# State space steps over pairs of groups, later row stores and earlier B and C loads in a hybrid decoder layer

## Chip, cores and metric

One core of a Trainium2 chip. The metric is the device time of one execution in microseconds (us). It was 2678.44 us before the change, the median of 3 runs (2677.90 to 2678.88).

## What is computed

One decoder layer on 2048 tokens of width 1024, in fp32. The input is normalised and projected by one matrix; the columns go to three mixers (sliding-window attention, a state space model, sparse attention). Their outputs are normalised, projected and added; a feed-forward block follows. The change touches the projection and the state space model alone:

```python
h = rms_norm(x, norm1_g[l]); proj = jnp.einsum('bld,de->ble', h, w_in[l])
# s5_mixer: 32 groups of 16 channels, 64 complex states per group
A_bar = jnp.exp(A * dt); B_bar = ((A_bar - 1.0) / A)[..., None] * Bm
Bu = jnp.einsum('blgp,gnp->blgn', uf, B_bar)
_, states = lax.associative_scan(_scan_combine, (a_seq, Bu), axis=1)
y = jnp.einsum('blgn,gpn->blgp', states, Cm).real + d_skip * uf
z = jax.nn.gelu(y)          # then a gated linear unit
```

## The kernel before

`phase_front` (L82) projects and runs the state space model; it ends at about 489 us, and attention and the rest follow. Sixteen blocks of 128 tokens are taken in two halves of eight. `load_h` loads and splits a block and starts a chain of 128x1 operations on POOL (L45 to L50), which gives the row scale r. `load_w` loads a chunk of weight columns in four pieces (wr, L130) and splits them on ACT (wh, L136) and DVE (wl, L137). `product` (L146) multiplies one block by one chunk: 24 matmuls into pm, three for each of 8 slices (`mm3`, L77 to L79). A product of a u chunk is scaled by r into u_st (L156). One of an a or c chunk goes to po (L160), with sums of squares beside it, and from there to memory at once (pa L166, pc L169); po has two buffers. pm has two buffers too, so PE opens a third product only when ACT has emptied the first.

In half 0 `ssm_tables` (L256) runs beside the products. It loads B (t_B, L371 to L374) and, two parts later, C (craw, L394 and L395, sixteen loads into four buffers), which PE transposes (L396). In half 1 the u products come first. Then `merge` (L65) interleaves 68 steps of the other chunks, most of them half a product of 12 matmuls, evenly with the 65 steps of `ssm_steps`. That order is written out: engines run their instructions in it, each waiting in its own queue.

`ssm_steps` (L414) works for each of the 32 groups g. On POOL `kernel_of` makes CA (L444 to L446, 128x272), an outer product of powers and C, for group g+2. PE then makes the local kernel pk (L448), which ACT and DVE copy to kst, and SP stores it (dkp, L453). `turned` loads CS (CA with its halves exchanged, L465, L466) and Wc (a shifted reading of dkp), and transposes B and u (pbt L481, pu L487). `scanned` multiplies into pv (L498); then DVE rotates (m, L501, L502) and scans (Q, L504), and POOL rotates back (St, L506). `answer` sums into py, two matmuls from Wc and two from St (L512 to L515), and gelu writes u_st (L516). For each g the order is turned(g+1), scanned(g), answer(g-1).

Of the kernel before, what the change touches and what calls it, by code (L numbers as in the profile page):

```python
# [16 lines left out]
P = 128  # L17
D = 1024
# [63 lines left out]
def phase_front(tc, C, x, norm1_g, w_in, u_st, pa, pc, rh_a, prm, dkp, extra):  # L82

    nc = tc.nc
    with ExitStack() as ctx:
# [15 lines left out]
        def load_h(s):  # L101
# [41 lines left out]
        def product(s, hs, w, kind, c0, n, part=None):  # L143
# [13 lines left out]
            else:  # L157
                f, nh = HEADS[c0]
                o = sp.tile([P, n + nh], F32, tag="po", name=f"po{s}_{c0}")
# [13 lines left out]
        for half in range(2):  # L173
# [14 lines left out]
            with tc.tile_pool(name=f"a_x{half}", bufs=2, reuse_waits="tile") as xp:  # L188
                box_x[:] = [xp]
                run(lists[0] + (lists[1] if half else []))  # L190
            if half == 0:
                with tc.tile_pool(name="bv", bufs=1) as bv:
                    extra(bv, ps_t)
                gen = ssm_tables(tc, C, S, kp, prm, dkp, ps_t)
                run(merge(sum(lists[1:], []), [lambda: next(gen, None)] * TABLE_PARTS + [lambda: None] * TABLE_REST))
            else:
                tp = ctx.enter_context(tc.tile_pool(name="sg", bufs=2))
                lists[4].insert(4, lambda: head_norms(nc, rh_a, *hn_tiles(sp, "hn"), pa, 256, 4, 516))
                rest = sum(lists[2:], [])
                run(merge(rest, ssm_steps(tc, C, S, u_st, dkp, tp, ps_g, ps_t)))  # L200

# [53 lines left out]
def ssm_tables(tc, C, S, pool, prm, dkp, ps):  # L255
# [12 lines left out]
    sn, cs = keep([P, 11, G], "sn"), keep([P, 11, G], "cs")  # L268
# [97 lines left out]
    with ExitStack() as ctx:  # L366
# [36 lines left out]
        dT = tmp([16, G], "dT")  # L403
        nc.sync.dma_start(dT, d_skip[0].rearrange("(g q) -> q g", q=16))
# [9 lines left out]
def ssm_steps(tc, C, S, u_st, dkp, tp, ps, ps_t):  # L414

    nc = tc.nc
    E, M, B = {}, {}, {}
    states = [tp.tile([P, 2, P], F32, name=f"St{j}", bufs=1) for j in range(2)]
    for t in states:
        nc.vector.memset(t[:, :, 0:1], 0.0)  # L420

    def tl(shape, n, g, bufs=None):
        return tp.tile(shape, F32, tag=n, name=f"{n}{g}", bufs=bufs)

    def turns(b):

        gs = slice(b * GB, b * GB + GB)
        e = E[b] = tl([P, 2, GB, P], "E", b)
        u1, u2 = tl([P, GB, 8, 16], "u1", b, 1), tl([P, GB, 8, 16], "u2", b, 1)
        ea = [S["Ea"][:, j, gs].unsqueeze(3).broadcast_to([P, GB, 8, 16]) for j in range(2)]  # L430
        eb = [S["Eb"][:, j, gs].unsqueeze(2).broadcast_to([P, GB, 8, 16]) for j in range(2)]
        o = [e[:, j].rearrange("p g (a b) -> p g a b", b=16) for j in range(2)]
# [23 lines left out]
    def turned(g):

        if g % GB == 0:
            turns(g // GB)
        for a in ((0, 1, 2) if g == 0 else (g + 2,)):  # L460
            if a < G:
                kernel_of(a)
        CA = M[g]
        CS, Wc = tl([P, 16, 16], "CS", g, 3), tl([P, 256], "Wc", g, 3)
        nc.sync.dma_start(CS[0:64], CA[64:P, 1:17])  # L465
        nc.sync.dma_start(CS[64:P], CA[0:64, 1:17])  # L466
        base = dkp[g]
        nc.sync.dma_start(Wc, bass.AP(base.tensor, base.offset, [[16, 8], [368, 16], [1, 256]]))
        M[g] = CA, CS, Wc
        if g % 2 == 0:  # L470
            bb = [P, 2, 16, 16]
            Bp, t2 = tl(bb, "Bp", g), tl(bb, "t2", g, 1)
            ar, ai = (S[n][:, 0:16, g:g + 2].rearrange("p t g -> p g t").unsqueeze(3).broadcast_to(bb) for n in ("AR", "AI"))
            nc.vector.tensor_tensor(Bp, ar, S["Y"][:, g:g + 2].unsqueeze(2).broadcast_to(bb), op=ALU.mult)
            nc.vector.tensor_tensor(t2, ai, S["W"][:, g:g + 2].unsqueeze(2).broadcast_to(bb), op=ALU.mult)
            nc.vector.tensor_tensor(Bp, Bp, t2, op=ALU.add)
            B[g], B[g + 1] = Bp[:, 0], Bp[:, 1]
        pb = ps.tile([P, 2, P], F32, tag="pb", name=f"pbt{g}", bufs=2)
        Bf = B.pop(g).rearrange("p a b -> p (a b)")
        for k in range(2):  # L480
            nc.tensor.transpose(pb[:, k], Bf[:, k * P:(k + 1) * P], C["ident"])  # L481
        BT = tl([P, 2, 192], "BT", g)
        nc.scalar.copy(BT[:, :, 0:P], pb)
        nc.scalar.copy(BT[:, :, P:192], pb[:, :, 0:64])
        pu = ps_t.tile([P, 2, P], F32, tag="pt", name=f"pu{g}")
        for k in range(2):
            nc.tensor.transpose(pu[:, k], u_st[:, g, k * P:(k + 1) * P], C["ident"])  # L487
        U = tl([P, 2, P], "U", g, 3)
# [20 lines left out]
    def answer(g):
        (U, St), (CA, CS, Wc) = M.pop(("y", g)), M.pop(g)  # L510
        py = ps.tile([P, 256], F32, tag="py", name=f"py{g}")
        nc.tensor.matmul(py, U[:, 1], Wc, start=True, stop=False)  # L512
        nc.tensor.matmul(py[:, P:256], U[:, 0], Wc[:, 0:P], start=False, stop=False)
        nc.tensor.matmul(py, St[:, 0], CA[:, 1:17].rearrange("p a b -> p (a b)"), start=False, stop=False)
        nc.tensor.matmul(py, St[:, 1], CS.rearrange("p a b -> p (a b)"), start=False, stop=True)  # L515
        nc.scalar.activation(u_st[:, g], py, AF.Gelu_apprx_tanh)  # L516
# [1277 lines left out]
```

## Time and profile before

| | us |
|---|---|
| median of 3 runs | 2678.44 |
| the profiled execution | 2676.44 |
| its span, first to last instruction | 2674.7 |
| PE busy in the span | 2515.1 (94%) |
| PE busy in 260 to 490 us | 205.37 of 230 |

Busy times are those of one engine; in a stage where PE has work in its queue, the time that the stage could lose is what PE waits. A wait is read from the engine that waits to the instruction that released it. "Triple" below is the time from one L77 to the next, which is three matmuls.

### The profile page before, as it was taken

The numbers are of one execution on the slowest core, as the hardware profiler recorded it, in microseconds if no ns is written. First come the engines' busy times: TensorE is split into PE (matmuls) and PEld (weight loads), VectorE is DVE, ScalarE is ACT, GpSimd is POOL, SyncE is SP. The second block draws the span as 40 slices with busy tenths as digits, with TensorE's granted clock in tenths as the row PEclk, the third lists the DMA queues.
The fourth block names the chain that finished last, engine by engine and source line by source line (L and its number), as shares of the span: only waits on it lengthen the run. The fifth ranks groups of instructions, "written<-read, shape, count | busy, mean of one in ns | idle before, by whom it ended". The sixth has DMA issues, their size and how long they took to land.

```text
span 2674.7 us, 39885 instructions
## 1 busy us (share of the span) xinstructions
PE 2515.1 (94%) x13480; PEld 2116.7 (79%) x13480; DVE 1787.5 (67%) x3476; ACT 1323.2 (49%) x2854; POOL 1136.4 (42%) x1257
## 2 busy tenths in 40 slices
PE   8998889899989999999969999989999999999999
PEld 7998878678767877777857777868887788888887
DVE  3834665565587677777756555676555788888886
ACT  5453333575466656655635545454445443444442
POOL 2013443322233333222246666666564354544447
PEclk9999999999989999999989999999999999999999
DMA  4352322522131111110136666675554744444435
GB/s 123 86 150 61 80 69 59 155 83 59 47 111 60 60 58 56 42 45 23 44 116 193 177 189 193 216 222 149 156 148 154 232 130 132 128 130 122 126 96 196
DMA packets 389677, 312.74 MB, mean 117 GB/s; under 512 B 55766, under 2 KB 358492, under 8 KB 387808
## 3 DMA queue, kind: packets, MB, share of 16 engines
q1 hardware_dynamic: 353376, 285.02, 35.9%
q10 hardware_dynamic: 36096, 25.17, 2.9%
q8 instruction: 107, 1.75, 0.3%
q14 instruction: 98, 0.80, 0.1%
HBM read 201.06 MB, written 104.85 MB: 114 GB/s over the span
## 4 chain that ended last, share of the span: by engine, by line
PE 59%; DVE 5%; DMA 4%; ACT 4%; POOL 3%; issue 2%; SPq 0%; ACTq 0%; DVEq 0%; POOLq 0%
PE pdc L1593 6%; PE puc L1431 6%; PE pda L1593 6%; PE pdb L1593 6%; PE pub L1431 5%; PE pua L1431 5%; PE pdd L1593 3%; PE pud L1431 3%; PE pw L77 2%; PE pps L822 2%; PE pos L830 2%; PE pw L79 2%; PE pw L78 2%; DMA vr<-vd 1%; PE pqs L801 1%
## 5 line engine op out<-in xcount | busy, mean ns | idle before, releaser
L1281 ACT CAST v<-vr 128x512 fp32r<-128x512 f32 x224 | 139.7, 624 | 308.8 <-DMA vr<-vd 164.5
L1282 DVE TENSOR_TENSOR v<-vr,v 128x512 fp32r<-128x512 f32 x224 | 234.7, 1055 | 76.7 <-ACT v L1281 74.6
L77 PE MATMUL pm<-wh,hh 128*128 128x256 f32 (+2 forms) x768 | 236.6, 309 | 8.9 <-ACT u_st L156 7.8
L78 PE MATMUL pm<-wl,hh 128*128 128x256 f32 (+2 forms) x768 | 226.9, 296 | 0.3 <-DVE wl L137 0.2
L79 PE MATMUL pm<-wh,hl 128*128 128x256 f32 (+2 forms) x768 | 225.4, 294 | 0.0
L1593 PE MATMUL pdc<-dw,v 128*128 128x512 f32 x768 | 185.3, 390 | 2.1 <-DVE acc L1614 1.8
L1593 PE MATMUL pda<-dw,v 128*128 128x512 f32 x768 | 185.0, 390 | 2.2 <-ACT dw L1281 1.5
L1593 PE MATMUL pdb<-dw,v 128*128 128x512 f32 x768 | 184.6, 389 | 0.1
L1593 PEld LDWEIGHTS pda<-dw,v 128*128 128x128 f32 x768 | 144.0, 188 | 33.2 <-ACT dw L1281 1.9
L1593 PEld LDWEIGHTS pdc<-dw,v 128*128 128x128 f32 x768 | 143.8, 188 | 33.4 <-DVE acc L1614 2.7
L1593 PEld LDWEIGHTS pdb<-dw,v 128*128 128x128 f32 x768 | 144.1, 188 | 30.3 <-issue 0.5
L1402 POOL TENSOR_TENSOR fs<-ur,ur 128x512 f32<-128x512 f32 x64 | 94.8, 1481 | 152.3 <-DMA ur<-in_w_up 139.2
L77 PEld LDWEIGHTS pm<-wh,hh 128*128 128x128 f32 x768 | 147.3, 192 | 12.3 <-ACT u_st L156 8.9
L1282 DVE TENSOR_TENSOR ul<-ur,uh 128x512 fp32r<-128x512 f32 x96 | 103.8, 1083 | 77.6 <-ACT uh L1281 77.6
L1281 ACT CAST uh<-fs 128x512 fp32r<-128x512 f32 x128 | 78.7, 622 | 154.4 <-PE pub L1431 61.7
L78 PEld LDWEIGHTS pm<-wl,hh 128*128 128x128 f32 x768 | 147.1, 192 | 4.6 <-issue 2.8
L79 PEld LDWEIGHTS pm<-wh,hl 128*128 128x128 f32 x768 | 146.8, 191 | 0.0
L1282 DVE TENSOR_TENSOR ul<-fs,uh 128x512 fp32r<-128x512 f32 x128 | 131.9, 1034 | 14.0 <-ACT uh L1281 13.7
L1431 PE MATMUL pua<-fh,uh 128*128 128x512 f32 x256 | 103.0, 402 | 23.3 <-ACT uh L1281 15.8
L1447 POOL TENSOR_TENSOR ev<-e,e 128x512 f32<-128x512 f32 x64 | 100.6, 1572 | 32.6 <-ACT e L1444 28.9
L77 PE MATMUL pw<-wo_h,mh 128*128 128x512 f32 x256 | 108.5, 424 | 4.3 <-ACT mh L1173 2.8
L826 DVE TENSOR_TENSOR tls<-pps,ths 128x512 fp32r<-128x512 f32 (+1 forms) x144 | 92.7, 657 | 28.2 <-ACT ths L825 19.4
(535 smaller groups left out, 7607.8 us busy)
## 6 DMA issues: line engine op xcount, KB each, us to landing
vr<-vd SPq DMA_DIRECT2D x224, 256.0 KB
ur<-in_w_up SPq DMA_DIRECT2D x128, 256.0 KB
vd<-ev SPq DMA_DIRECT2D x128, 256.0 KB
vd<-e ACTq DMA_DIRECT2D x64, 256.0 KB
dr<-in_w_down SPq DMA_DIRECT2D x32, 512.0 KB
wr<-in_w_in SPq DMA_DIRECT2D x40, 256.0 KB
x<-in_x SPq DMA_DIRECT2D x16, 512.0 KB
mx<-in_x SPq DMA_DIRECT2D x16, 512.0 KB
```

Of the source, the lines that this page charges most:

```text
L77: nc.tensor.matmul(out, sh, mh, start=first, stop=False)
L78: nc.tensor.matmul(out, sh, ml, start=False, stop=False)
L79: nc.tensor.matmul(out, sl, mh, start=False, stop=last)
L822: nc.tensor.transpose(pt[:, j, hh], sls[hh][:, (b0 + j) * P:(b0 + j + 1) * P], C["ident"])
L826: nc.vector.tensor_tensor(tl[:, 0:nb], pt[:, 0:nb], th[:, 0:nb], op=ALU.subtract)
L830: nc.tensor.matmul(po, v_of(b0 + j), t[:, j].rearrange("p h q -> p (h q)"), start=b0 + j == 0 and n == 0, stop=b0 + j == nblk - 1 and n == 1)
L1281: nc.scalar.copy(dh, src)
L1282: nc.vector.tensor_tensor(dl, src, dh, op=ALU.subtract)
L1402: nc.gpsimd.tensor_tensor(t, x, y, op=op)
L1431: nc.tensor.matmul(bank[b], w[:, k], h[o][:, k], start=first and k == 0 and n == 0, stop=k == HALF - 1 and n == 2, skip_group_check=True)
L1447: nc.gpsimd.tensor_tensor(tile_("v" + o), x, y, op=op)
L1593: nc.tensor.matmul(bank[b, q], x[:, q, j], y[:, j], start=first and j == 0 and n == 0, stop=j == 1 and n == 2, skip_group_check=True)
```

## The change

It does six things. (1) Every operation of the state space steps takes a pair b of groups: CA, t and m are 544 or 512 wide, pk, pv, py and the transposes are issued for both groups in a row, and one gelu, one dkp store, one pair of CS loads and one St (a single tile) serve both. (2) The steps of a pair are scanned(b), turned(b+1), answer(b), and scanned(b) begins with pk of b+1 (`local`). CA of b+2 is made after answer(b); three pairs of CA are made at the start. There are 49 steps instead of 65 among the 68. (3) A row store is kept in a list and issued when the next product has been written; po has three buffers. (4) All sixteen C loads, into eight buffers, and the load of dT are issued with the B loads, one part ahead of B's first use. (5) The temporaries of the row scale come from the pool of x, whose reuse in half 1 is tracked otherwise. (6) `head_norms` stands four steps later.

```diff
@@ product
-                if kind == "a":
-                    o0 = c0 // 256 * 260
-                    nc.sync.dma_start(pav[s, :, o0:o0 + n + nh], o)
...
+                rows.append(lambda: nc.sync.dma_start(dst[s, :, o0:o0 + n + nh], o))
+                store(1)
@@ phase_front
-            with tc.tile_pool(name=f"a_x{half}", bufs=2, reuse_waits="tile") as xp:
+            with tc.tile_pool(name=f"a_x{half}", bufs=2, **({} if half else {"reuse_waits": "tile"})) as xp:
...
-                lists[4].insert(4, lambda: head_norms(nc, rh_a, *hn_tiles(sp, "hn"), pa, 256, 4, 516))
+                lists[4].insert(8, lambda: head_norms(nc, rh_a, *hn_tiles(sp, "hn"), pa, 256, 4, 516))
@@ ssm_tables, behind the B loads
+        for a, b in ((cr, ci), (ci, cr)):
+            for j in range(4):
+                raw = raws[id(a), j] = tp.tile([P, 2, 64], F32, tag="craw", name="craw", bufs=8)
+                nc.sync.dma_start(raw[:, 0], a[j * P:(j + 1) * P])
+                nc.sync.dma_start(raw[:, 1], b[j * P:(j + 1) * P])
+        dT = tmp([16, G], "dT")
+        nc.sync.dma_start(dT, d_skip[0].rearrange("(g q) -> q g", q=16))
+        yield
@@ ssm_steps
-    states = [tp.tile([P, 2, P], F32, name=f"St{j}", bufs=1) for j in range(2)]
+    St = tp.tile([P, GB, 2, P], F32, name="St")
...
+    def outer(b):
+        bc = [P, GB, 17, 16]
+        CA, t1 = tl(bc, "CA", b, 3), tl(bc, "t1", b)
...
+    def scanned(b):
+        if b + 1 < NB:
+            local(b + 1)
...
+        nc.vector.tensor_tensor(m, pv, e, op=ALU.mult)
+        nc.vector.tensor_tensor(m[:, :, 0], m[:, :, 0], m[:, :, 1], op=ALU.add)
+        Q = tl([P, GB, P], "Q", b)
+        for i in range(GB):
+            g = b * GB + i
+            nc.vector.tensor_tensor_scan(Q[:, i], S["rho16"][:, g:g + 1].to_broadcast([P, P]), m[:, i, 0], 0.0, op0=ALU.mult, op1=ALU.add)
+        n = P - 1
+        nc.gpsimd.tensor_tensor(St[:, :, :, 1:P], Q[:, :, 0:n].unsqueeze(2).broadcast_to([P, GB, 2, n]), e[:, :, :, 0:n], op=ALU.mult)
...
+    def first():
+        outer(0)
+        outer(1)
+        local(0)
+    res = [first, lambda: turned(0)]
+    for b in range(NB):
+        res.append(lambda b=b: scanned(b))
+        if b + 1 < NB:
+            res.append(lambda b=b: turned(b + 1))
+        res.append(lambda b=b: answer(b))
```

POOL at the end of the row scales of half 1. Before, the last block's chain (rqh, r, L45 to L50) stands between the first CA operations:

```order
L45 TENSOR_SCALAR rqh<-ss_2804 128x1
L444 TENSOR_TENSOR CA_3174<-k_AR,k_C_716 128x272
L46 TENSOR_SCALAR r_2806<-rqh 128x1
L445 TENSOR_TENSOR t_3175<-k_AI,k_C_717 128x272
L49 TENSOR_SCALAR rqt<-r_2806,rqh 128x1
L444 TENSOR_TENSOR CA_3185<-k_AR,k_C_716 128x272
```

And now:

```order
L49 TENSOR_SCALAR rqt<-r_2805,rqh 128x1
L50 TENSOR_SCALAR r_2805<-rqt,r_2805 128x1
L455 TENSOR_TENSOR CA_3162<-k_AR,k_C_716 128x544
L456 TENSOR_TENSOR t_3163<-k_AI,k_C_717 128x544
L455 TENSOR_TENSOR CA_3167<-k_AR,k_C_716 128x544
L457 TENSOR_TENSOR CA_3162<-CA_3162,t_3163 128x544
```

The chain is now whole, and stands ahead of every CA operation.

POOL amid the state space steps. Before, with one CA and one St for a group:

```order
L445 TENSOR_TENSOR t_3484<-k_AI,k_C_717 128x272
L444 TENSOR_TENSOR CA_3483<-k_AR,k_C_716 128x272
L506 TENSOR_TENSOR St_3121<-Q_3452,E_3310 128x2x127
L446 TENSOR_TENSOR CA_3483<-CA_3483,t_3484 128x272
L445 TENSOR_TENSOR t_3564<-k_AI,k_C_717 128x272
```

And now, one of each for a pair:

```order
L456 TENSOR_TENSOR t_3508<-k_AI,k_C_717 128x544
L522 TENSOR_TENSOR St<-Q_3276,E_3192 128x4x127
L455 TENSOR_TENSOR CA_3507<-k_AR,k_C_716 128x544
L457 TENSOR_TENSOR CA_3507<-CA_3507,t_3508 128x544
L456 TENSOR_TENSOR t_3642<-k_AI,k_C_717 128x544
```

CA's last operation (L446, now L457) no longer has an St between it and its first. The pair of pk that reads CA_3507 comes two answers later on PE.

SP in half 0, from the last B load. Before, two stores of rows (pa) stand ahead of the sixteen C loads:

```order
L374 DMA t_B_1542<-in_ssm_b_re 64x32x16
L166 DMA pa<-po_256_1705 128x258
L166 DMA pa<-po_256_1736 128x258
L394 DMA craw<-in_ssm_c_re 128x64
L395 DMA craw<-in_ssm_c_im 128x64
```

And now, from the last two C loads:

```order
L385 DMA craw<-in_ssm_c_im 128x64
L386 DMA craw<-in_ssm_c_re 128x64
L388 DMA t_dT<-in_ssm_d 16x32x1
L165 DMA pa<-po_256_1730 128x258
L165 DMA pa<-po_256_1761 128x258
L165 DMA pc<-po_1024_1849 128x325
```

The two stores have moved behind all sixteen loads and that of dT.

## Rows read from the trace of the kernel before

**Rows 1.** Stretches of the span: from and to, length, busy time of PE, PEld, DVE, ACT and POOL (with the instructions), granted TensorE clock as a share of full speed, DMA share, GB/s.
```profile
212.00:246.00 34.00, 26.20 (x182) 25.73 (x181) 10.97 (x24) 7.33 (x17) 11.73 (x17) 0.85 0.17 44
260.00:490.00 230.00, 205.37 (x1381) 191.37 (x1380) 130.06 (x289) 76.88 (x226) 90.49 (x129) 0.99 0.27 71
490.00:530.00 40.00, 27.96 (x134) 19.65 (x132) 26.88 (x75) 26.35 (x72) 16.85 (x27) 0.87 0.69 201
```
**Rows 2.** Waits from 246 to 490 us: engine and line that waited, what released it, us in total, times, longest.
```profile
PE pk L448 <- POOL CA L446: 23.9, 24, 4.5
PE pbt L481 <- ACT kst L452: 1.0, 2, 0.5
```
**Rows 3.** The longest of these: the timeline of PE (start, duration, instruction, idle time before it), then stretches as in rows 1.
```profile
370.13 0.31 PE L77 MATMUL pm<-wh,hh 128*128 128x320 f32 x1
370.57 0.31 PE L77 MATMUL pm<-wh,hh 128*128 128x320 f32 x1
375.67 1.22 PE L448 MATMUL pk<-CA,k_Y 128*128 128x256 f32 x2 [4.50 <-POOL CA L446]
...
375.00:380.00 5.00, 4.33 (x16) 3.96 (x17) 0.63 (x3) 1.03 (x4) 1.93 (x3) 0.50 0.01 4
380.00:385.00 5.00, 5.00 (x28) 4.58 (x28) 3.96 (x8) 1.38 (x3) 3.19 (x4) 0.84 0.20 52
```
**Rows 4.** The timeline of one group: PE, DVE and POOL.
```profile
300.41 0.38 PE L481 MATMUL pbt<-c_ident,Bp 128*128 128x128 f32 x2
300.77 0.37 PE L77 MATMUL pm<-wh,hh 128*128 128x256 f32 x1
302.27 1.05 PE L498 MATMUL pv<-U,BT 128*128 128x128 f32 x8
303.16 0.60 PE L512 MATMUL py<-Wc,U 128*128 128x256 f32 x2
...
303.76 0.41 DVE L501 TENSOR_TENSOR m<-pv,E 128x256 f32<-128x256 f32 x1
306.30 0.89 DVE L504 TENSOR_TENSOR_SCAN Q<-k_rho,m 128x128 f32<-128x128 f32 x1
307.27 0.73 POOL L506 TENSOR_TENSOR St<-Q,E 128x254 f32<-128x254 f32 x1 [0.36 <-DVE Q L504]
```
**Rows 5.** Groups of instructions from 246 to 490 us: busy time, mean ns of one, idle time before them and its releasers.
```profile
L504 DVE TENSOR_TENSOR_SCAN Q<-k_rho,m 128x128 f32<-128x128 f32 x32 | 16.1, 503 | 1.1
L476 DVE TENSOR_TENSOR Bp<-Bp,t 128x512 f32<-128x512 f32 x14 | 9.6, 687 | 0.2
L435 DVE TENSOR_TENSOR E<-u,u 128x256 f32<-128x256 f32 x14 | 11.9, 848 | 13.1 <-POOL St L506 13.1
L433 DVE TENSOR_TENSOR u<-k_Ea,k_Eb 128x256 f32<-128x256 f32 x13 | 5.6, 434 | 0.4
```
**Rows 6.** POOL's two-input operations of 128x512: one in the timeline at 503 us, and a group of the whole span.
```profile
503.51 1.04 POOL L744 TENSOR_TENSOR qda<-ta,rh_a 128x512 f32<-128x512 f32 x1
...
L1402 POOL TENSOR_TENSOR fs<-ur,ur 128x512 f32<-128x512 f32 x64 | 94.8, 1481 | 152.3 <-DMA ur<-in_w_up 139.2
```
**Rows 7.** The timeline at the end of the u products of half 1: PE, ACT, POOL and SP's queue (SPq).
```profile
212.71 0.28 PE L77 MATMUL pm<-wh,hh 128*128 128x256 f32 x1
218.01 0.58 PE L77 MATMUL pm<-wh,hh 128*128 128x256 f32 x1 [4.78 <-ACT u_st L156]
225.58 0.58 PE L77 MATMUL pm<-wh,hh 128*128 128x256 f32 x1 [3.03 <-ACT u_st L156]
...
217.48 0.47 ACT L156 ACTIVATE u_st<-pm,r 128x256 f32<-128x256 f32 x1 [7.77 <-POOL r L50]
223.81 1.36 ACT L136 ACTIVATE wh<-wr,g 128x256 fp32r<-128x256 f32 x3 [5.86 <-DMA wr<-in_w_in]
...
202.79 0.19 POOL L45 TENSOR_SCALAR rqh<-ss 128x1 f32<-128x1 f32 x1 [0.54 <-ACT x L118]
205.42 0.27 POOL L50 TENSOR_SCALAR r<-rqt,r 128x1 f32<-128x1 f32 x1
206.52 0.43 POOL L45 TENSOR_SCALAR rqh<-ss 128x1 f32<-128x1 f32 x1 [0.83 <-ACT x L118]
217.18 0.26 POOL L50 TENSOR_SCALAR r<-rqt,r 128x1 f32<-128x1 f32 x1
...
220.30 0.46 SPq L465 DMA_DIRECT2D CS<-CA  x1
220.80 1.13 SPq L130 DMA_DIRECT2D wr<-in_w_in  x2
```
**Rows 8.** Around the C loads: a wait from 118 to 150 us, as in rows 2, then the timelines of ACT and SP's queue.
```profile
PE p L396 <- DMA craw<-in_ssm_c_im: 2.6, 1, 2.6
...
126.53 0.53 ACT L160 ACTIVATE po<-pm,r 128x320 f32<-128x320 f32 x1 [5.75 <-DMA pa<-po]
...
123.37 1.56 SPq L166 DMA_DIRECT2D pa<-po  x2
124.98 0.45 SPq L394 DMA_DIRECT2D craw<-in_ssm_c_re  x1
132.12 0.43 SPq L395 DMA_DIRECT2D craw<-in_ssm_c_re  x1
```
**Rows 9.** PE's longest wait from 480 to 530 us, as in rows 2.
```profile
PE ptqa L751 <- POOL qda L744: 5.8, 2, 5.4
```

More of the change, by code (lines that the diff above doesn't have):

```diff
@@ L416, in ssm_steps, with tl, of @@
     nc = tc.nc
-    E, M, B = {}, {}, {}
-    states = [tp.tile([P, 2, P], F32, name=f"St{j}", bufs=1) for j in range(2)]
[L419 to L423, printed above, removed]
-    def turns(b):
[L427 to L432, printed above, removed]
+    M = {}
+    St = tp.tile([P, GB, 2, P], F32, name="St")
+    nc.vector.memset(St[:, :, :, 0:1], 0.0)
+    NB = G // GB
+    def tl(shape, n, b, bufs=1):
+        return tp.tile(shape, F32, tag=n, name=f"{n}{b}", bufs=bufs)
+    def of(b):
+        return slice(b * GB, b * GB + GB)
+    def turns(b):
+        e = M["e", b] = tl([P, GB, 2, P], "E", b, 2)
+        u = tl([P, 2, GB, 8, 16], "t2", f"u{b}")
+        u1, u2 = u[:, 0], u[:, 1]
+        ea = [S["Ea"][:, j, of(b)].unsqueeze(3).broadcast_to([P, GB, 8, 16]) for j in range(2)]
+        eb = [S["Eb"][:, j, of(b)].unsqueeze(2).broadcast_to([P, GB, 8, 16]) for j in range(2)]
+        o = [e[:, :, j].rearrange("p g (a b) -> p g a b", b=16) for j in range(2)]
         nc.vector.tensor_tensor(u1, ea[0], eb[0], op=ALU.mult)
@@ L456, in turned @@
[L456 to L488, printed above, removed]
-        nc.scalar.copy(U, pu)
-        M["b", g] = BT, U
@@ L509, in answer @@
[L509 to L516, printed above, removed]
@@ new lines, in local @@
+    def local(b):
+        CA = M["c", b]
+        pk = ps.tile([P, GB, 256], F32, tag="pb", name=f"pk{b}", bufs=2)
+        for i in range(GB):
+            g = b * GB + i
+            nc.tensor.matmul(pk[:, i], S["Yp"][:, g:g + 8].rearrange("p a b -> p (a b)"), CA[:, i, 0:16].rearrange("p a b -> p (a b)"),
+                             start=True, stop=True)
+        kst = tl([16, GB, 256], "kst", b)
+        nc.vector.tensor_tensor(kst[:, :, 0:16], pk[0:16, :, 0:16], S["dD"][:, of(b)], op=ALU.add)
+        nc.scalar.copy(kst[:, :, 16:256], pk[0:16, :, 16:256])
+        nc.sync.dma_start(dkp[of(b), :, 112:368].rearrange("g q c -> q g c"), kst)
@@ new lines, in turned @@
+    def turned(b):
+        turns(b)
+        CA = M["c", b]
+        CS, Wc = tl([P, GB, 16, 16], "CS", b, 2), tl([P, GB, 256], "Wc", b, 2)
+        nc.sync.dma_start(CS[0:64], CA[64:P, :, 1:17])
+        nc.sync.dma_start(CS[64:P], CA[0:64, :, 1:17])
+        for i in range(GB):
+            base = dkp[b * GB + i]
+            nc.sync.dma_start(Wc[:, i], bass.AP(base.tensor, base.offset, [[16, 8], [368, 16], [1, 256]]))
+        bb = [P, GB, 16, 16]
+        Bp, t2 = tl(bb, "Bp", b), tl(bb, "t2", b)
+        ar, ai = (S[n][:, 0:16, of(b)].rearrange("p t g -> p g t").unsqueeze(3).broadcast_to(bb) for n in ("AR", "AI"))
+        nc.vector.tensor_tensor(Bp, ar, S["Y"][:, of(b)].unsqueeze(2).broadcast_to(bb), op=ALU.mult)
+        nc.vector.tensor_tensor(t2, ai, S["W"][:, of(b)].unsqueeze(2).broadcast_to(bb), op=ALU.mult)
+        nc.vector.tensor_tensor(Bp, Bp, t2, op=ALU.add)
+        pb = ps.tile([P, GB, 2, P], F32, tag="pb", name=f"pbt{b}", bufs=2)
+        pu = ps_t.tile([P, GB, 2, P], F32, tag="pt", name=f"pu{b}")
+        for i in range(GB):
+            for k in range(2):
+                nc.tensor.transpose(pu[:, i, k], u_st[:, b * GB + i, k * P:(k + 1) * P], C["ident"])
+        U = tl([P, GB, 2, P], "U", b, 2)
+        nc.scalar.copy(U, pu)
+        for i in range(GB):
+            for k in range(2):
+                nc.tensor.transpose(pb[:, i, k], Bp[:, i, 8 * k:8 * k + 8].rearrange("p a b -> p (a b)"), C["ident"])
+        BT = tl([P, GB, 2, 192], "BT", b)
+        nc.scalar.copy(BT[:, :, :, 0:P], pb)
+        nc.scalar.copy(BT[:, :, :, P:192], pb[:, :, :, 0:64])
+        M["b", b] = BT, U, CA, CS, Wc
@@ new lines, in scanned @@
+    def scanned(b):
+        if b + 1 < NB:
+            local(b + 1)
+        BT, U = M["b", b][0:2]
+        pv = ps.tile([P, GB, 2, P], F32, tag="pv", name=f"pv{b}")
+        for i in range(GB):
+            for j in range(2):
+                for k in range(2):
+                    nc.tensor.matmul(pv[:, i, j], BT[:, i, k, 64 * j:64 * j + P], U[:, i, k], start=k == 0, stop=k == 1)
+        m, e = tl([P, GB, 2, P], "m", b), M.pop(("e", b))
+        nc.vector.tensor_tensor(m, pv, e, op=ALU.mult)
+        nc.vector.tensor_tensor(m[:, :, 0], m[:, :, 0], m[:, :, 1], op=ALU.add)
+        Q = tl([P, GB, P], "Q", b)
+        for i in range(GB):
+            g = b * GB + i
+            nc.vector.tensor_tensor_scan(Q[:, i], S["rho16"][:, g:g + 1].to_broadcast([P, P]), m[:, i, 0], 0.0, op0=ALU.mult, op1=ALU.add)
+        n = P - 1
+        nc.gpsimd.tensor_tensor(St[:, :, :, 1:P], Q[:, :, 0:n].unsqueeze(2).broadcast_to([P, GB, 2, n]), e[:, :, :, 0:n], op=ALU.mult)
@@ new lines, in answer @@
+    def answer(b):
+        _, U, CA, CS, Wc = M.pop(("b", b))
+        py = ps.tile([P, GB, 256], F32, tag="py", name=f"py{b}")
+        for i in range(GB):
+            nc.tensor.matmul(py[:, i], U[:, i, 1], Wc[:, i], start=True, stop=False)
+            nc.tensor.matmul(py[:, i, P:256], U[:, i, 0], Wc[:, i, 0:P], start=False, stop=False)
+            nc.tensor.matmul(py[:, i], St[:, i, 0], CA[:, i, 1:17].rearrange("p a b -> p (a b)"), start=False, stop=False)
+            nc.tensor.matmul(py[:, i], St[:, i, 1], CS[:, i].rearrange("p a b -> p (a b)"), start=False, stop=True)
+        nc.scalar.activation(u_st[:, of(b)], py, AF.Gelu_apprx_tanh)
+        if b + 2 < NB:
+            outer(b + 2)
```

72 lines of the change are left out of this document (19 added, 53 removed).

## The prediction

> **What bounds the kernel now.** I read the busy times by stretch first. PE works 2515 of 2675 us, so what PE does not wait for changes the end little, and the question is what PE waits for in the front phase. From 260 to 490 us, where the state space steps run beside the products, PE is busy 205.37 of 230 us; from 212 to 246 it is busy 26.20 of 34, at a granted clock of 0.85 [rows 1]. The waits say on what. Between 246 and 490 us nearly all of PE's idle time is pk waiting for the last of CA's three POOL operations: 23.9 us in 24 waits. Beside it stands 1.0 us of pbt on ACT [rows 2]. The longest of the 24 is 4.50 us, and behind it the granted clock is 0.50 for 5 us, the lower of its two levels (1.2 and 2.4 GHz), and 0.84 for 5 more [rows 3]. CA comes late because its three operations are split around an St, in a queue that waits for PE and DVE in turn. Before 246 us PE stands twice at the end of the u products, 4.78 and 3.03 us, both times for ACT's scaling of u_st: ACT waited 7.77 us for the row scale r of POOL, then 5.86 us for weights [rows 7]. At 127 us there is one wait of 2.6 us for C [rows 8]. The stage that follows, 490 to 530 us, has PE busy for only 28 of 40 us and DMA for 0.69 of it [rows 1], with 5.8 us of waiting for qda [rows 9].
>
> **The change, part by part.** The number of multiplications does not change; each term below is idle time or time at the lower clock.
>
> *A. Around the C loads.* Before, two row stores are issued ahead of them (1.56 us) and then sixteen loads at about 0.48 us, from 124.98 to 132.55; PE waits 2.6 us [rows 8]. Now the loads follow B directly and start 1.6 us sooner. But PE reaches the first transpose of C 7 matmuls sooner (1.0 us at a triple of 0.44 [rows 3]), so about 2 us of wait stay: gain 0.6. The two stores now stand behind sixteen loads and dT, some 8 us later. ACT's next po but one needs that buffer; it already waited 5.75 us for such a store [rows 8]. The third buffer covers one product of 24 matmuls (8 x 0.44 = 3.5 us), pm's second one some 2.5 more, so I charge the 2 us that are left to PE. **A = -1.5**, bounds -4 (the store is late by 8, covered by 3.5) and +2.7 (both waits go).
>
> *B. The end of the u products.* The last row scale takes from 206.52 to 217.18 because CA operations stand between its links. The chain itself needs 2.9 us: the one before ran from 202.79 to 205.69 without them. Whole and ahead of CA it ends at about 209.4, before the product that needs it is finished (PE's last triple starts at 212.71), so the 4.78 us go. The second wait was for weights issued at 220.80, behind a CS load [rows 7], and landed at 223.81, 3.0 us later. Now only the CS of pair 0 stands ahead, which waits for CA(0). This is the fourth POOL operation after r. Each is 544 wide; I take 1.5 us, from the 1.04 and 1.48 of 512-wide ones [rows 6]: 209.4 + 4 x 1.5 = 215.4, a CS issue, weights issued at 216.2, landed at 219.2. ACT splits them (1.36 us [rows 7]) and u_st follows; PE resumes at about 221.1, against 225.58 [rows 7]. The work between the two stops is done before the second instead; the lower clock behind it I leave as it was. **B = +4.5**, bounds +2.5 (CA at 2 us each) and +6.3 (CA at 1.04).
>
> *C. 246 to 490 us.* CA of a pair is made two answers ahead of its pk, so the 23.9 us and the 1.0 us [rows 2] go; what covers CA is a whole pair of PE work, some 13 us, against 4.5 us on POOL. Gone too is the lower clock behind the long wait: 5 us at half speed and 5 at 0.84 lose 2.5 + 0.8, less 0.35 of idle time in them: 2.95 us [rows 3]. Together 27.9.
> What is late next is St. Before, group g's St had a group of PE work before py read it. Now py of pair b reads it in the same round as pv: pv, then 12 or 24 matmuls, eight transposes, 12 or 24 matmuls, two py matmuls from Wc, then St. This cover is worked out from one group's timeline: 12 matmuls take 1.5 us (300.77 to 302.27), four transposes 0.4, the Wc part 0.65 [rows 4]: 1.5 + 0.8 + 1.5 + 0.65 = 4.4 us where there are two runs of 12, and 5.9 with one of 24. At 320 and 332 columns (1.75 and 1.82 for 12) it is 4.9 to 6.9. By the order on PE three pairs have 4.4, one 4.6, two about 5, eight 5.7 or more; pair 9 has only 3.2 and the last 2.5. The chain against it: m of 512 at 0.69 (by Bp of that width), its sum at 0.43 (by u), two scans at 0.50 [rows 5], St at 1.04 to 1.48 [rows 6], 0.3 between them: 3.5 to 3.9. Operations of two inputs on DVE do take twice as long at times: E 848 ns against u's 434 [rows 5]; twice the 2.1 us on DVE and the longer St give 6.0. I take 4.4: waits of 1.2 in pair 9 and 1.9 in the last, 3.1 in all. **C = +25**, bounds +28 (the chain always covered) and +17 (chain 5.5: 3 x 1.1 + 0.9 + 1 + 2.3 + 3.0 = 10.5).
> Queues passed: on SP the CS loads of a pair wait for CA, made early, and Wc waits for its dkp store; weight loads stand behind them, but are needed a chunk later. ACT's copies are twice as wide and half as many.
>
> *D. 490 to 530 us.* The second qda moves ahead of the head norm chain on POOL and the loads of ta ahead of the others. Of the 5.8 us of waiting for qda [rows 9] some goes, but a weight load of 1 MB now stands ahead of the GLU's weights in a stage with DMA at 0.69 [rows 1]. **D = +2**, bounds -4 and +5.8.
>
> The later order on every engine is the same. The stores and `head_norms` steps after 246 us have a round of slack each: 0.
>
> **Sum**: -1.5 + 4.5 + 25 + 2 = 30. The profiled execution took 2676.44 us, 2.0 below the median of the runs, 2678.44. So 2646.4 in a profile, and 2648.4, say **2648**, as a median. With all bounds added it is +11.5 to +42.8.
>
> **The rivals.**
> *R1, slower: St's chain sets each round.* The chain of a single group took from pv's end at 303.16 to 308.00, 4.8 us, with two weight splits of DVE in it [rows 4]. Doubled in all its parts that is 9.6 us, in every one of 16 pairs. The waits then sum: at 7 us of chain 3 x 2.6 + 2.4 + 4 x 1.3 + 5 + 8.3 = 28.7 (the 5 from the six rounds of 5 to 6.9, the 8.3 from pair 9 and the last), all of C's 27.9; that is the point where it decides. At 8 us another 16 come: C = -17, the sum -12, time 2690. Against it: only m, its sum and St grow, by 0.27, 0.1 and 0.5 us, and one scan of 0.50 is added, 1.4 us in all; the splits stand in few rounds.
> *R2, half of it.* The chain lies at 6, through the contention of rows 5. The waits are 3 x 1.6 + 1.4 + 1.9 + 4 x 0.2 + 2.8 + 3.5 = 15.2 and C = +12.7; sum 17.7, time 2661. The Trainium skill, "GPSIMD Engine Reference", section "Specifications", states that POOL's SBUF interface is shared with VectorE, with contention when a DVE instruction has two SBUF inputs: a rule against wider POOL work beside DVE. The 848 against 434 ns agree with it for one form, but no row shows it at 512.
> *R3, given back at the boundary.* PE reaches 490 some 28 us sooner, but the next stage's loads are issued behind the last steps and are limited by DMA. D is -8: 2658. For it: 0.69 of DMA; against: most of these loads move with SP's queue, which is sooner too.
> *R4, the wait stays under another name.* CA(b+2) still waits for py(b-1), the CS loads for CA, and py for CS. If CS lands late by as much as CA did, C is near +2 and the time about 2672 to 2685. Against: CS is loaded a round before its py.
>
> **How the numbers follow.** No change means within 0.2%, 5.4 us, about what a measurement of this kernel can tell. Forecast 0.66, R1 0.09 (0.02 of it between), R2 0.12, R3 0.08, R4 0.05 (half of it slower). The forecast's own range is 2636 to 2667. The range 2634 to 2670 takes in R2 and R3 and leaves out R1, R4 and the ends, about 0.2. Faster is the forecast, R3 and most of R2: 0.84; same 0.07; slower, R1 and part of R4: 0.09.
>
> **What would show it.** Right: no wait of pk on CA; py waiting for St for 2 to 5 us in all, in pair 9 and the last; no wait of u_st on r, PE back at about 221; granted clock 1.00 through the steps; the last product near 461 us; a wait of C at 125 of about 2 us and one of pm on ACT near 132. It is wrong if py waits for St in most rounds, if a new wait on CS or Wc stands in PE's list, or if PE's idle time between 490 and 530 grows by more than 4 us.

## The result and the profile after

The changed kernel takes 2647.17 us (median of 4 runs, 2645.72 to 2648.50) against 2678.66 before (4 runs). The ratio is 0.9883, with a 95% interval of 0.9866 to 0.9900. Timed again later (e9), it took 2645.21 us against 2680.94, ratio 0.9863 (0.9849 to 0.9878). The forecast was 2648.

Three landmarks split the profiled executions: the first pk, before which every kernel here has issued the same 1536 product matmuls; the last py; the end of the span. The two rows of each kernel list the 64 matmuls of pk and the 64 of the last of py's four lines: shortest, median and longest in ns, then the start of the first and of the last in us. First before, then after:

```profile
L448 PE MATMUL pk<-CA,k_Y x64: 378/379/796, 245.4 to 461.4; 128*128 128x256 f32 x64
L515 PE MATMUL py<-CS,St x64: 379/379/507, 259.7 to 486.6; 128*128 128x256 f32 x64
```
```profile
L466 PE MATMUL pk<-CA,k_Y x64: 377/379/380, 245.9 to 438.6; 128*128 128x256 f32 x64
L531 PE MATMUL py<-CS,St x64: 378/379/634, 259.3 to 459.6; 128*128 128x256 f32 x64
```

| us | before | after | gain | forecast |
|---|---|---|---|---|
| to the first pk (A, B) | 245.4 | 245.9 | -0.5 | +3.0 |
| first pk to last py (C) | 241.2 | 213.7 | +27.5 | +25 |
| last py to the end (D) | 2188.1 | 2187.1 | +1.0 | +2 |
| span | 2674.7 | 2646.7 | +28.0 | +30 |

So the sum holds, and the way to it less well. (The B loads, which the title calls earlier, keep their place on SP: the first is issued at 119.41 us, at 118.48 before. Only those of C and dT moved.)

In the state space steps PE now hardly stands. The stretches from the first pk to the last py, before and then after (columns as in rows 1):

```profile
245.38:486.98 241.60, 216.73 (x1464) 201.66 (x1462) 137.15 (x306) 84.07 (x245) 90.72 (x129) 0.99 0.28 72
```
```profile
245.87:459.98 214.11, 208.84 (x1464) 200.98 (x1463) 137.76 (x263) 76.40 (x165) 77.89 (x71) 0.99 0.33 84
```

The same 1464 matmul records take 208.84 us instead of 216.73, and PE's idle time falls from 24.87 to 5.27. No wait of pk is left [rows 2]; the waits of PE from 235 to 462 us are one line:

```profile
PE py L530 <- POOL St L522: 5.1, 3, 3.5
```

Its three waits are in pairs 8, 9 and 15. Pair 9 is the one with a short cover, and its timeline shows the chain that the forecast priced, on PE, DVE and POOL:

```profile
371.14 1.95 PE L513 MATMUL pv<-U,BT 128*128 128x128 f32 x16
...
377.00 0.70 PE L530 MATMUL py<-CA,St 128*128 128x256 f32 x2 [0.62 <-POOL St L522]
...
373.13 0.69 DVE L515 TENSOR_TENSOR m<-pv,E 128x512 f32<-128x512 f32 x1 [1.60 <-PE pv L513]
373.86 0.42 DVE L516 TENSOR_TENSOR m<-m 128x256 f32<-128x256 f32 x1
374.20 0.69 DVE L486 TENSOR_TENSOR Bp<-k_AR,k_Y 128x512 f32<-128x512 f32 x1
374.80 0.73 DVE L520 TENSOR_TENSOR_SCAN Q<-k_rho,m 128x128 f32<-128x128 f32 x2
...
375.68 1.27 POOL L522 TENSOR_TENSOR St<-Q,E 128x508 f32<-128x508 f32 x1 [5.22 <-DVE Q L520]
```

From pv's end (373.09) to St's (376.95) it is 3.9 us, the upper end of the 3.5 to 3.9 worked out and below the 4.4 taken. Its parts differ: the two scans take 0.73 us together where 1.0 was counted, and a Bp of 0.69, which wasn't counted, stands among them. The longest wait, 3.48 us, is in pair 8, whose cover is long. POOL shows why, PE's wait beside it:

```profile
355.35 0.44 POOL L45 TENSOR_SCALAR hnhn<-hnhn 128x96 f32<-128x96 f32 x1 [3.72 <-DMA hnhn<-pa]
...
360.96 0.39 POOL L55 TENSOR_TENSOR rh_a<-rh_a,hnhn 128x96 f32<-128x96 f32 x1
361.30 1.26 POOL L522 TENSOR_TENSOR St<-Q,E 128x508 f32<-128x508 f32 x1
...
362.61 0.70 PE L530 MATMUL py<-CA,St 128*128 128x256 f32 x2 [3.48 <-POOL St L522]
```

St stands behind the fourteen operations of the head norms, which themselves waited 3.72 us for their load; Q had been ready since 356.45. Behind the stop the granted clock is 0.50 for 3.4 us (363.4 to 366.8).

The kernel before has the same stop under another name. Its longest wait of pk, 4.50 us until 375.67 [rows 3], was laid to the St between CA's operations. POOL shows the head norms there, between t and the rest of CA:

```profile
364.79 0.67 POOL L445 TENSOR_TENSOR t<-k_AI,k_C 128x272 f32<-128x272 f32 x1
367.00 0.50 POOL L45 TENSOR_SCALAR hnhn<-hnhn 128x96 f32<-128x96 f32 x1 [1.54 <-DMA hnhn<-pa]
...
373.77 0.39 POOL L55 TENSOR_TENSOR rh_a<-rh_a,hnhn 128x96 f32<-128x96 f32 x1
374.11 0.67 POOL L444 TENSOR_TENSOR CA<-k_AR,k_C 128x272 f32<-128x272 f32 x1
374.86 0.76 POOL L446 TENSOR_TENSOR CA<-CA,t 128x272 f32<-128x272 f32 x1
```

The other 23 waits are 1.73 us at most. So the longest, and the 6.8 us at clock 0.50 behind it (374.8 to 381.6), stood behind a chain that the change moves by four steps but doesn't shorten.

At the end of the u products (PE, DVE, POOL and SP's queue), to be read against rows 7:

```profile
217.48 0.39 PE L78 MATMUL pm<-wl,hh 128*128 128x256 f32 x1 [1.49 <-DVE wl L137]
...
227.41 0.58 PE L77 MATMUL pm<-wh,hh 128*128 128x256 f32 x1 [3.58 <-ACT u_st L156]
...
212.81 0.42 DVE L443 TENSOR_TENSOR t2u<-k_Ea,k_Eb 128x256 f32<-128x256 f32 x1 [3.24 <-ACT wh L136]
...
218.82 1.39 DVE L445 TENSOR_TENSOR E<-t2u 128x256 f32<-128x256 f32 x1
220.13 2.88 DVE L137 SCALAR_TENSOR_TENSOR wl<-wr,g,wh 128x256 fp32r<-128x256 f32 x2
...
218.58 1.34 POOL L455 TENSOR_TENSOR CA<-k_AR,k_C 128x544 f32<-128x544 f32 x1
...
219.38 4.04 SPq L130 DMA_DIRECT2D wr<-in_w_in  x2
```

The wait for r is gone, as forecast, and weights are issued at 219.38 instead of 220.80. But the second piece follows only at some 223, since its buffer is given back by wl, and wl takes 1.4 us a piece on DVE.

Around the C loads, the stretch before and after, then PE and ACT after, against rows 8:

```profile
125.00:150.00 25.00, 22.62 (x156) 22.51 (x157) 11.29 (x20) 8.74 (x18) 0.00 (x0) 1.00 0.66 169
125.00:150.00 25.00, 21.57 (x139) 21.29 (x140) 10.59 (x19) 6.15 (x14) 0.00 (x0) 0.93 0.54 128
...
128.19 0.45 PE L405 MATMUL p<-c_ident,craw 128*128 128x128 f32 x1 [3.27 <-DMA craw<-in_ssm_c_im]
...
135.89 0.41 PE L77 MATMUL pm<-wh,hh 128*128 128x320 f32 x1 [0.24 <-ACT po L160]
...
135.31 1.03 ACT L160 ACTIVATE po<-pm,r 128x320 f32<-128x320 f32 x2 [11.35 <-DMA pa<-po]
```

ACT waits 11.35 us for the stores that moved behind the loads, but only 0.24 of it reaches PE. The wait for C grows to 3.27, and the granted clock of the stretch falls from 1.00 to 0.93.

One stop was not in the forecast at all. At 41 us PE waits 1.4 us for a small load (boh), in front of which SP had waited for the last row scale of half 0. PE's wait before and after, then SP's wait after (30 to 45 us):

```profile
PE bpr L622 <- DMA boh<-in_k_oh: 0.7, 1, 0.7
PE bpr L641 <- DMA boh<-in_k_oh: 1.4, 1, 1.4
SPq L634 <- POOL r L50: 3.0, 1, 3.0
```

Before, SP does not wait for r there. By the code it does now since edit 5 puts the temporaries of the row scale into the pool of x, whose space the next loads take over; no run undoes edit 5 alone. Behind the stop the granted clock is 0.50 for 3.4 us (42.5 to 45.9).

### The profile page after: what moved, and what is told of

Its sections match the earlier page's. It is cut to its first block, busy times and chain, and to the rows that moved or that the text cites. A ratio compares the mean times of both kernels' runs of the same rounds, so it can differ in the third digit from the quotient of the medians.

```text
span 2646.7 us, 39486 instructions
## 1 busy us (share of the span) xinstructions
PE 2505.8 (95%) x13480; PEld 2116.4 (80%) x13480; DVE 1796.4 (68%) x3427; ACT 1315.2 (50%) x2774; POOL 1124.1 (42%) x1193
## 5 line engine op out<-in xcount | busy, mean ns | idle before, releaser
L77 PE MATMUL pm<-wh,hh 128*128 128x256 f32 (+2 forms) x768 | 233.9, 305 | 5.4 <-ACT u_st L156 3.6
L79 PE MATMUL pm<-wh,hl 128*128 128x256 f32 (+2 forms) x768 | 227.0, 296 | 0.0
L1612 PEld LDWEIGHTS pda<-dw,v 128*128 128x128 f32 x768 | 144.0, 188 | 33.3 <-ACT dw L1300 2.7
L1612 PEld LDWEIGHTS pdc<-dw,v 128*128 128x128 f32 x768 | 143.9, 188 | 33.3 <-DVE acc L1633 2.8
L77 PEld LDWEIGHTS pm<-wh,hh 128*128 128x128 f32 x768 | 147.9, 193 | 8.4 <-ACT u_st L156 3.8
L79 PEld LDWEIGHTS pm<-wh,hl 128*128 128x128 f32 x768 | 147.5, 192 | 0.1
L1450 PE MATMUL pua<-fh,uh 128*128 128x512 f32 x256 | 103.7, 405 | 24.9 <-ACT uh L1300 15.7
L77 PE MATMUL pw<-wo_h,mh 128*128 128x512 f32 x256 | 109.3, 427 | 4.4 <-ACT mh L1192 2.8
L845 DVE TENSOR_TENSOR tls<-pps,ths 128x512 fp32r<-128x512 f32 (+1 forms) x144 | 92.7, 657 | 28.5 <-ACT ths L844 21.8
```

Of the source, the lines that this page charges most:

```text
L77: nc.tensor.matmul(out, sh, mh, start=first, stop=False)
L79: nc.tensor.matmul(out, sl, mh, start=False, stop=last)
L845: nc.vector.tensor_tensor(tl[:, 0:nb], pt[:, 0:nb], th[:, 0:nb], op=ALU.subtract)
L1450: nc.tensor.matmul(bank[b], w[:, k], h[o][:, k], start=first and k == 0 and n == 0, stop=k == HALF - 1 and n == 2, skip_group_check=True)
L1612: nc.tensor.matmul(bank[b, q], x[:, q, j], y[:, j], start=first and j == 0 and n == 0, stop=j == 1 and n == 2, skip_group_check=True)
```

## The experiments

All times in us; landmarks from the profiled execution, medians of 4 runs (e2: 10).

| kernel | first pk | last py | between | span | median |
|---|---|---|---|---|---|
| before | 245.4 | 486.6 | 241.2 | 2674.7 | 2678.66 |
| changed | 245.9 | 459.6 | 213.7 | 2646.7 | 2647.17 |
| e9, changed again | 246.8 | 457.6 | 210.8 | 2642.4 | 2645.21 |
| e1 pairs only | 245.4 | 458.6 | 213.2 | 2641.4 | 2641.97 |
| e2 all but pairs | 246.1 | 487.2 | 241.1 | 2673.5 | 2675.23 |
| e3 e2 and CA ahead | 245.7 | 460.4 | 214.7 | 2648.7 | 2650.52 |
| e8 before and CA ahead | 244.6 | 462.3 | 217.7 | 2652.4 | 2654.09 |
| e4 old C loads | 248.9 | 459.0 | 210.1 | 2644.7 | 2645.71 |
| e5 narrow CA | 244.9 | 455.1 | 210.2 | 2643.2 | 2645.87 |
| e6 norms later | 249.1 | 456.4 | 207.3 | 2642.8 | 2643.94 |
| e7 e1 and norms later | 240.6 | 448.1 | 207.5 | 2633.6 | 2639.53 |
| e10 e7 and narrow CA | 245.0 | 452.5 | 207.5 | 2631.0 | 2638.14 |
| e11 changed, e4 to e6 | 242.8 | 450.2 | 207.4 | 2635.6 | 2637.09 |

Medians are to be compared beside the kernel before of the same set: 2677.66 beside e1 to e4, 2679.68 beside e5 to e8, 2680.94 beside e9 to e11. Executions of one kernel scatter (e10: 2632.80 to 2643.49). The first pk came at 245.9, 246.8 and 249.1 in three kernels with the same instructions up to it (changed, e9, e6). The column between is steadier, but not exact: 213.7, 210.8 and 210.1 in three with the same steps (changed, e9, e4).

The front phase can be split further by counting the product matmuls (L77 to L79): the 577th starts near 94 us, the 1345th near 212, the 1536th is the last before pk. The range of each stretch in the executions profiled:

| us | front phase as before (before, e1, e7, e8, e10) | changed front phase (changed, e9, e2 to e6, e11) |
|---|---|---|
| to the 577th product | 92.8 to 95.9 | 94.5 to 98.1 |
| 577th to 1345th (A) | 116.1 to 118.2 | 118.6 to 120.1 |
| 1345th to the first pk (B), one group at a time | 35.2 to 35.5 | 30.6 to 30.9 |
| the same, pairs | 31.7 to 33.6 | 29.4 to 33.3 |

**e1, pairs alone.** The new `ssm_steps` in the old front phase (sn and cs as temporaries, to fit). The changed kernel's other edits are undone, such as

```diff
-                rows.append(lambda: nc.sync.dma_start(dst[s, :, o0:o0 + n + nh], o))
-                store(1)
...
+                if kind == "a":
+                    o0 = c0 // 256 * 260
+                    nc.sync.dma_start(pav[s, :, o0:o0 + n + nh], o)
...
```

> The state space steps over pairs alone, in the front phase of the kernel before (loads of C, row stores, temporaries of the row scale, place of the head norms as before). Theory: the wait of pk on CA is what was won, and pairs remove it by themselves: no wait of pk on CA, C = +28 us; the C loads cost nothing more (+2.2 against the changed kernel); the last row scale is still split by CA operations, now 544 wide at 1.4 us, so it ends near 219 and PE stands some 7 us for it. In all about 2650 us. Rival (the front parts carry part of the gain): 2660 or more.

No wait of pk, and C is as large as with the whole change. PE stands once for u_st, 6.7 us, as expected; the first pk comes no later than with the whole row scale. The median is 5.2 below the changed kernel's (3.2 below e9's), where 3 more were expected: the forecast of 2650 missed by 8. But e1's ratio to the kernel before beside it, 0.9863 (0.9840 to 0.9885), is that of e9, so it isn't shown to be faster than the whole change, only not slower. At the last py it is within 1 us of both; the rest of the difference lies in the stages behind, in the same order of instructions, and stays open.

**e2, all but the pairs.** The old `ssm_steps` in the changed front phase; against the kernel before:

```diff
-                lists[4].insert(4, lambda: head_norms(nc, rh_a, *hn_tiles(sp, "hn"), pa, 256, 4, 516))
+                lists[4].insert(8, lambda: head_norms(nc, rh_a, *hn_tiles(sp, "hn"), pa, 256, 4, 516))
...
-                if kind == "a":
...
+                rows.append(lambda: nc.sync.dma_start(dst[s, :, o0:o0 + n + nh], o))
+                store(1)
```

> Everything of the change but the pairs: one group at a time as before. Theory: pk waits for CA 20 to 26 us as before, PE waits about 3.3 us for C with a lower clock behind it (-2.2), the row scale is whole (+3 to +4): 2675 to 2679 us. Rival (later stores and the third row buffer help the steps too): 2665 or less.

Ratio 0.9987 (0.9977 to 0.9998), 2675.23 us, as the theory has it. pk waits as ever, and nothing else of C moves:

```profile
PE pk L455 <- POOL CA L453: 24.0, 25, 4.5
```

**e3 and e8, CA one group further ahead.** One group at a time; e3 is e2 with the making of CA (`outer_of`) moved, e8 the kernel before with it, and a few buffers shared to fit.

```diff
+AHEAD = 1
...
-        CA, t1 = tl(bc, "CA", g, 5), tl(bc, "t1", g, 1)
+        CA, t1 = tl(bc, "CA", g, AHEAD + 5), tl(bc, "t1", g, 1)
...
+        if g == 0:
+            for a in range(2 + AHEAD):
+                outer_of(a)
         for a in ((0, 1, 2) if g == 0 else (g + 2,)):
             if a < G:
                 kernel_of(a)
+        if g + 2 + AHEAD < G:
+            outer_of(g + 2 + AHEAD)
```

> As the kernel with everything but the pairs, and CA made one group further ahead of its pk (six CA buffers; the temporaries of the rotation share a buffer with another of DVE, to fit). One group at a time. Theory (how early CA is made is all that matters): the wait of pk on CA goes, no wait of py on St comes, 2648 to 2652 us. Rival (fewer, wider operations matter): pk still waits for half, 2660 or more.

> The kernel before with CA made one group further ahead and nothing else (two buffers shared or given back earlier, to fit). Theory: the wait of pk goes as in e3 and the front parts cost nothing here: 2645 to 2649 us. Rival (the front parts are needed, for the row scale): 2651 or more.

Without any pair the wait of pk is gone and 26.5 of the 27.5 us are won (e3), 23.5 in the old front phase (e8). So the gain is that CA is made earlier. Pairs are one way to it; in the changed kernel, too, an St still stands between t and the other two operations of CA (t at 369.21, St at 375.68, CA at 379.30); only the lead is longer. No run has pairs without the lead. PE's busy time falls in e3 too, for the same 1464 records (216.43 us in e2):

```profile
245.70:460.80 215.10, 209.26 (x1464) 199.47 (x1463) 134.75 (x307) 83.66 (x246) 80.61 (x114) 0.99 0.32 82
```

What the busy time gave goes with the stops, then, not with the width. Two forecasts missed here. py does wait for St, 3.1 us in e3 and 4.1 in e8, at 364 us, where the head norms stand. And e8's 2654.09 lies in its rival's range, not the theory's. B shows what the rival had right: with one group at a time the changed front phase saves some 4.6 us there (35.2 and 35.5 against 30.6 and 30.9). The front parts lose most of it again ahead of B (the first two rows of the table above).

**e4, the C loads where they were**, behind B's part, in four buffers.

```diff
-                raw = raws[id(a), j] = tp.tile([P, 2, 64], F32, tag="craw", name="craw", bufs=8)
...
+                raw = tp.tile([P, 2, 64], F32, tag="craw", name="craw", bufs=4)
+                nc.sync.dma_start(raw[:, 0], a[j * P:(j + 1) * P])
+                nc.sync.dma_start(raw[:, 1], b[j * P:(j + 1) * P])
```

> The changed kernel with the C loads and dT issued where they were before, four buffers. Theory: the changed place costs 2.2 us, from a longer wait for C and a lower clock behind it; so 2645 us, and PE's 96th product slice after 96 us is reached 2 us sooner. Rival (the loss is the later row store): no change, 2647.

The wait for C is 3.0 us, hardly shorter, and A takes 120.1 us, no less than with the moved loads. So the theory falls: the place of the loads isn't what costs. The rival, that putting them back changes nothing, fits the stretch; that its cause is the later row store is not shown, since no run undoes that alone. What the traces do show is that A is longer in each of the eight executions with the changed front phase than in any of the five with the old one. Part of that is the lower clock behind a stop, which comes and goes: from 110 to 150 us the stop for C was 2.6 us at clock 1.00 before, 2.6 at 0.96 in e1, 2.3 at 1.00 in e7, and 3.5 at 1.00 in e3.

**e5, narrow CA.**

```diff
-        nc.gpsimd.tensor_tensor(CA, ar, S["C1"][:, of(b)].unsqueeze(2).broadcast_to(bc), op=ALU.mult)
...
+        for i in range(GB):
+            nc.gpsimd.tensor_tensor(CA[:, i], ar[:, i], c1[:, i], op=ALU.mult)
+            nc.gpsimd.tensor_tensor(t1[:, i], ai[:, i], c2[:, i], op=ALU.mult)
+            nc.gpsimd.tensor_tensor(CA[:, i], CA[:, i], t1[:, i], op=ALU.add)
```

> The changed kernel with each of CA's three POOL operations split in two, one for each group of the pair (272 wide). Theory: a DVE operation on two SBUF operands waits out the POOL operation that is running, so the weight splits and rotations of DVE between 212 and 227 us take 0.7 to 0.9 us instead of 1.4, PE's 2.3 us on wl go, and it is back 1 to 2 us sooner; 2645 to 2647 us. Rival (the two share bandwidth, whatever the width): DVE's operations stay near 1.4 us, POOL's nine operations only gain start costs, 2647 to 2649.

The timeline of DVE at the same place, and POOL's operation that was running when E began:

```profile
217.28 0.89 DVE L445 TENSOR_TENSOR E<-t2u 128x256 f32<-128x256 f32 x1
218.10 1.80 DVE L137 SCALAR_TENSOR_TENSOR wl<-wr,g,wh 128x256 fp32r<-128x256 f32 x2
...
217.04 0.86 POOL L458 TENSOR_TENSOR t<-k_AI,k_C 128x272 f32<-128x272 f32 x1
```

E takes 0.89 instead of 1.39, a weight split 0.9 instead of 1.4, and PE's waits for wl fall from 2.3 to 0.3. PE's whole idle time in B is 4.6 us, and 4.3 in e11, where the four kernels with wide CA behind the changed front phase have 5.5 to 5.9. The first pk is 1.0 sooner than the changed kernel's, which is within the scatter, and the median, 2645.87, doesn't tell the two apart.

**e6, the head norms held back**, behind St of pair 11:

```diff
-                lists[4].insert(8, lambda: head_norms(nc, rh_a, *hn_tiles(sp, "hn"), pa, 256, 4, 516))
+                lists[5].insert(2, lambda: head_norms(nc, rh_a, *hn_tiles(sp, "hn"), pa, 256, 4, 516, S["St"][:, 0, 0, 1:2]))
...
+    if behind is not None:
+        nc.gpsimd.tensor_scalar(tmp[0][:, 0, 0:1], behind, 1.0, 0.0, op0=ALU.mult, op1=ALU.add)
     rsqrt_steps(nc.gpsimd, r, ss, *tmp, 1.0 / 64)
```

> The changed kernel with the head norm chain of fourteen POOL operations held behind St of pair 11 by a small operation that reads St (its result isn't used). Theory: that chain, waiting for its load, stands ahead of St of pair 8 and costs 3.5 us of PE and the lower clock behind it; both go: 2642 to 2643.5 us, py waits for St about 2 us in all. Rival (the stop at pair 8 is the St chain itself): the stop stays and moves by nothing, 2647.

py waits for St once, 1.0 us, in the last pair, and the stretch where the stop was is full. First the changed kernel's, then that of e6:

```profile
350.00:365.00 15.00, 11.52 (x75) 10.87 (x74) 8.62 (x18) 3.40 (x8) 7.69 (x17) 0.95 0.26 51
350.00:365.00 15.00, 15.00 (x103) 14.47 (x102) 13.29 (x25) 5.58 (x13) 5.85 (x5) 1.00 0.42 94
```

The steps take 207.3 us, 3.5 less than in e9 and 6.4 less than in the changed kernel's first profile. The median is 2643.94, 3.2 below the changed kernel's, with overlapping ratios (0.9865, 0.9849 to 0.9882). The stop is the head norms' doing wherever they stand: it is there, 3.1 to 4.1 us, in e1, e3 and e8, and gone in all four kernels that hold them back.

**e7, e10 and e11, together.**

> The pairs alone in the front phase of the kernel before, with the same hold on the head norms. Theory: both gains add up, 2642 less 4.7, about 2637 us. Rival (what e1 won over the whole change came from the place of the head norms): 2642.

> e7 (pairs in the front phase of the kernel before, head norms held back) with CA's operations narrow as in e5. Theory: DVE's waits on POOL halve, PE is back 1 us sooner at the end of the u products: first pk at 240 to 244 us, last py 207 to 208 us behind it, 2636 to 2639 us. Rival (the row scale, split by more operations, ends later): 2640 or more.

> The changed kernel with its three losses mended: C loads in their old place (e4), narrow CA (e5), head norms held back (e6). Theory: 2647 less 2 (C loads), 1 (narrow) and 4.7 (head norms): 2639 to 2641 us. Rival (e1 and e7 show that the whole row scale and the loads' place win nothing): equal to e10 within 2 us, or above it.

> The changed kernel once more, beside the two below on one chip. Theory (executions of one kernel scatter by some us in the stages behind 460 us): again 2645 to 2650 us, the first pk at 245 to 247 us and the last py near 460. Rival (what separates e1 from the changed kernel is chance of the execution): below 2643.

All three take 207.4 to 207.5 us for the steps. e7's median, 2639.53, lies between its theory (2637) and its rival (2642), with runs from 2635.39 to 2642.22; that the wait went is clear, the size of the gain in the whole time isn't. e11 gives 2637.09, ratio 0.9834 (0.9820 to 0.9849): each of its runs (2636.34 to 2639.80) is faster than each of the changed kernel's beside it (e9, 2643.81 to 2647.37). Its median is 8.1 lower, e10's 7.1. e11 is below its theory's range and within 2 us of e10, as its rival says: the whole row scale and the place of the loads aren't shown to win anything once CA is narrow and the head norms are held back. e10's first pk came at 245.0, not by 244: two stops (6.5 us in all) where e7 had one. Narrow CA on top of e7 isn't shown to win anything. The rival of e9 is not borne out: the changed kernel took 2647 and then 2645.

## Why the prediction was right, point by point

The total came within 1 us of 2648 partly by luck: the start of the front phase lost what no term had, B and A gave less than forecast, and C more.

- **C, +27.5 for +25** (+30.4 by e9's profile, above the bound of +28). The mechanism is shown: early CA (e3) or pairs, which bring it (e1), remove the wait; the rest (e2) removes nothing. Two steps in it were off, in opposite ways. "The stores and `head_norms` steps after 246 us have a round of slack each: 0" failed: the head norms cost 3.5 us and the clock behind it (e6). The price stood in the trace before: the 4.50 us and the lower clock that were put down to the St between CA's operations stood behind the head norms. And the stops cost more than their idle time. PE's idle time fell by 19.6 us, less than the 21.8 that the forecast has (24.9 less 3.1 for St), but its busy time fell by 7.9, where the forecast had only the 2.95 at the lower clock. pk itself had a mean of 431 ns before and has 378 now. The St chain was sized well (3.9 us for 4.4), and its waits in pairs 9 and 15 are 0.62 and 1.04 (for 1.2 and 1.9).
- **The start, -1.1, where the forecast has no term.** The 577th product starts at 94.94 us, before at 93.86. The stop for boh is there in all eight kernels with the changed front phase, 1.3 or 1.4 us each; those with the old one wait 0.7 at most. The part on the change named edit 5, but no term priced it.
- **B, +2.9 for +4.5**, near its lower bound of +2.5. r is whole and its wait gone; the failed step is "ACT splits them (1.36 us [rows 7]) and u_st follows". Beside 544-wide POOL operations the DVE half of the split takes 1.4 us, and the next weight load waits for it. e5 shows it. With one group at a time the same front parts win about 4.6 us (e2, e3); with pairs they aren't shown to win anything (e1, e7).
- **A, -2.3 for -1.5.** Close by chance: the loads start 1.1 us sooner (1.6 expected) and the wait for C is 3.3 us (2 expected); the ACT wait hardly reaches PE (0.24 for 2; 1.5 in e3); and the clock, not in the sum, takes the rest.
- **D, +1.0 for +2.** As forecast, the wait for qda falls, from 5.8 to 3.0 us; a wait that the kernel before does not have stands beside it. D is +5.3 in e1 and +3.3 in e9, with the same order behind; a term of this size can't be told from scatter. The two waits of PE (461 to 503 us):

```profile
PE gpm L607 <- DVE glu_bh L581: 3.3, 1, 3.3
PE ptqa L770 <- POOL qda L763: 3.0, 1, 3.0
```

- **The rivals.** R1 would need a chain of 7 us; it has 3.9. R2's contention exists, but where DVE meets a row of CA operations, not in the chain. R3: what PE won by the last py, 27.0 us, is there at the end, 28.0. R4: no wait on CS or Wc appears among PE's waits.

## What to carry to other kernels

When a short wait recurs, ask how early its producer could be issued before widening anything: one more buffer and one step's lead gave 26.5 of 27.5 us. A long chain on an in-order engine (here the head norms, with a late load at its head) delays whatever stands behind it, so price every step that is moved onto a shared queue. Look also at what ran on DVE beside a POOL operation before widening it: here a weight split took 0.9 us beside the narrow operations and 1.4 beside the wide ones. And ask what releases the space when a tile moves into another pool: here the next loads were held back by 3.0 us.

## What was not expected of the hardware

A DVE operation on two SBUF operands that ran amid a row of POOL operations took about as long as one of those. E of 128x256 took 0.42 us by itself, 0.89 beside POOL operations of 272 (0.85 to 1.13 us in e5) and 1.39 beside those of 544 (1.2 to 1.6 us). In both cases it ended shortly after the POOL operation that was running when it began, 0.27 and 0.29 us behind it, so the delay here went with the POOL operation's width. The Trainium skill, "GPSIMD Engine Reference", section "Specifications", names contention of the two engines for DVE instructions with two SBUF inputs; the runs agree, and add the size.
